# Matmul operands on the left of SBUF, and the norms' two steps a chunk apart, in a two-layer hybrid encoder

## The chip, the cores and the metric

One NeuronCore of a Trainium2 chip runs the whole program. The metric is device time in microseconds (us), from the first to the last instruction of a launch, and the figure for a kernel is the median of its runs.

## What is computed

The reference is an encoder of two layers on 512 tokens of 1024 channels, in float32. Layer 0 mixes the tokens with RWKV-7 and Hyena, layer 1 with neighbourhood attention. Behind each mixer come a gated feed-forward part and a gated per-layer embedding. The parts that the change touches:

```python
def rmsnorm(x, g):
    xf = x.astype(jnp.float32)
    y = xf * lax.rsqrt(jnp.mean(xf * xf, axis=-1, keepdims=True) + EPS)
    return (y * g.astype(jnp.float32)).astype(x.dtype)

def conv_ffn(h, norm_g, w_up, conv_w, conv_b, w_down):
    u = dwconv_centred(rmsnorm(h, norm_g) @ w_up, conv_w, conv_b)
    return (jax.nn.gelu(u[..., :D_FF]) * u[..., D_FF:]) @ w_down

def per_layer_embedding(h, p_i, norm_g, w_gate, w_proj):
    return jax.nn.sigmoid(rmsnorm(h, norm_g) @ w_gate) * (p_i @ w_proj)

# in reference(), for each layer i
    z = rmsnorm(h, na_norm[j]) @ na_w_qkv[j]                      # layer 1's mixer
    h = h + neighbourhood_attention(z, na_q_g[j], na_k_g[j], na_rpb[j]) @ na_w_out[j]
    h = h + conv_ffn(h, ffn_norm[i], ffn_w_up[i], ffn_conv_w[i], ffn_conv_b[i], ffn_w_down[i])
    h = h + per_layer_embedding(h, p[i], ple_norm[i], ple_w_gate[i], ple_w_proj[i])
```

## The kernel before

**Stages.** `run` (L475) does layer 0's mixer (`mixer0`), then the second part of its output projection (`outproj0`, L1551), `ffn(0)`, `ple(0)`, `mixer1`, `ffn(1)` and `ple(1)`. The residual stream stays in SBUF as eight tiles `h` of 128 channels by 512 tokens. The mixer of layer 0 works in 59 slabs `w` of 2,080 bytes per partition and leaves `h_d` in DRAM, from which `outproj0` loads `h` (L1553).

**Every product in float32r.** Each operand is split in two parts, high and low, and a product is three matmuls (`mm3`, L370): high by high, high by low, low by high. `split` (L361) makes the high part on ScalarE and the low part on VectorE. Of the activations the parts are `xh`/`xl` (normed input), `hh`/`hl` (the feed-forward's hidden tiles) and `oh`/`ol` (attention's output); of the weights `whi`/`wlo`.

**Weights in chunks.** `load_split` (L375) brings 512 KB from DRAM into `wraw`, casts `whi` on ScalarE (L364) and subtracts `wlo` on VectorE (L356). Three buffers each. `gemm` (L384) takes four output tiles at a time and, per chunk, two row tiles of weights: 4 x 2 x 3 = 24 matmuls of 512 columns. The weights are stationary and the activations stream. In `gemm_tok` (L1631, attention's queries, keys and values) it is the other way round: `xh`/`xl` are stationary and `whi`/`wlo` stream.

**The norms.** `norm` (L435) splits `gain * h` at once, and 1/rms is applied where a product leaves PSUM (`u<-g,rstd`). The factor is computed while the first product runs, by `then()`, which `gemm` calls after its second chunk (L406): four matmuls add the squares `nacc` over the channels, VectorE scales (`rv`), GpSimd takes the power (`rr`), ScalarE spreads the result along a row (`rex`), TensorE transposes it four times (L431) and ScalarE copies `rstd` (L459). In `mixer1` the sums stand ahead of the first product (L1673 to L1677) and no transposes are needed.

**What sets the order.** Tile's scheduler puts each engine's instructions in one order ahead of time, and each engine runs its own strictly in that order. Loads go through SyncE's queue (SP), in one order too: a load whose place in SBUF is still being read holds up all that stand behind it.

**Where tiles lie.** Pools are stacks that grow from the two ends of SBUF; `side` says from which. Worked out from the sizes and the order in which pools open, in KB per partition from the bottom, with what the change makes of it:

| tiles | before | changed |
|---|---|---|
| `xh`, `xl` | 19.8 to 51.8 | the same |
| `wraw` | 51.8 to 63.8 | 212.0 to 224.0 |
| `whi` | 63.8 to 75.8 | 51.8 to 63.8 |
| `wlo` | 75.8 to 87.8 | 63.8 to 75.8 |
| `oh`/`ol`, eight pairs in turn | 101.7 to 133.7 | 75.8 to 107.8 |
| `hh`, twelve | 160.0 to 184.0 | 75.8 to 99.8 |
| `hl`, twelve | 184.0 to 208.0 | 99.8 to 123.8 |
| `h` | 208.0 to 224.0 | 183.8 to 199.8 |
| norm's tiles (`nsq`, `nacc`, `rstd`, `rex`) | 87.8 to 100.0 | 199.8 to 212.0 |
| slabs `w` of the mixer of layer 0 | 104.1 to 224.0 | the same |

The stages share this space one after the other, and a tile's first writer waits for the last reader of what lay there.

Of the kernel before, what the change touches and what calls it, by code (L numbers as in the profile page):

```python
# [10 lines left out]
F32 = mybir.dt.float32  # L11
# [21 lines left out]
# ---------------------------------------------------------------- layout of the weights  # L33
# [14 lines left out]
# row tiles of layer 0's output projection: those of its early part, and the others  # L48
# [20 lines left out]
def _kc(n):  # L69
    """Row tiles of weights in a chunk of n column tiles."""  # L70
    return (8, 4, 2, 2)[n - 1]
# [13 lines left out]
# columns of the packed per-channel parameters: name -> number of columns  # L85
# [32 lines left out]
# ---------------------------------------------------------------- constants of the shapes  # L118
# [23 lines left out]
def _constants():  # L142
# [18 lines left out]
    # transforms at the frequencies (2f+1)pi/1024, f < 256; even and odd times apart, which gives those of 511 - f  # L161
# [4 lines left out]
    fwd = parts.reshape(4, 4, P, 2, P)  # part, tile of times, time, fc, f  # L166
    c["dft_f"] = np.ascontiguousarray(fwd.transpose(3, 2, 0, 1, 4)).reshape(2, P, 2048)
    inv = parts.transpose(0, 2, 1).reshape(4, 2, P, S)  # part, fc, f, time
    c["dft_i"] = np.ascontiguousarray(inv.transpose(1, 2, 0, 3)).reshape(2, P, 2048)
    # filter features and decay window  # L170
# [10 lines left out]
def _rpb_table(rpb):  # L181
    """Relative position bias as each (16-column query block, head) reads it, both by columns of the grid;
    -1e30 outside the window."""
# [16 lines left out]
    t = np.stack(out, axis=2).reshape(8, 2, P, 3, 256)  # pair, head, q, table, key  # L200
# [3 lines left out]
# ---------------------------------------------------------------- the kernel  # L204
class Pace:
    """Estimates of when what is written so far will have run. The order in which the rest is written follows them;
    nothing that is computed depends on them."""
# [16 lines left out]
    def area(x):  # L224
        """Name, first and last row, first and last column."""
# [16 lines left out]
    def ready(self, tiles):  # L242
        """When all that is written into the tiles so far is there."""
        self.update()
        return max((math.inf if self.pending.get(n) else max(self.done.get(n, {}).values(), default=0.0)
                    for n in map(self.name, tiles)), default=0.0)

    def after(self, marks, area, e, own):
        """The end of the accesses in marks to an area, seen by engine e; those of its own count only if own."""
# [10 lines left out]
    # TensorE runs at half its clock after a stretch of this many us in which it streamed less than so many columns  # L260
# [5 lines left out]
    def density(self, t):  # L266
        """Columns streamed in the last TICK us before t."""
# [48 lines left out]
class Kern:  # L316
# [5 lines left out]
    # -- helpers  # L322
# [38 lines left out]
    def split(self, h, l, src, scale=None):  # L361
        """h + l = src (* scale), each in float32r."""
# [12 lines left out]
    def load_split(self, src, width, dt=F32):  # L375
        """One chunk of weights: from DRAM and into its two parts."""
# [7 lines left out]
    def gemm(self, wname, g, k0, k1, xs, evac, then=None):  # L384
        """then: what goes in between after two chunks of weights."""
# [6 lines left out]
        for kc in range(k0, k1, KC):  # L392
# [13 lines left out]
            if then is not None and kc == k0 + KC:  # L406
                then()

    def rsqrt_rows(self, pool, srcs, col, scale, eps):
        """For each of srcs [128 channels, tokens]: 1 / sqrt(scale * (sums over the channels of col) + eps),  # L410
        back on all of those channels, in PSUM."""
        nc = self.nc
        n = col.shape[1]
        w = 4 * n
        ps = self.pm.tile([P, len(srcs) * w], F32, name="m")
        for i, src in enumerate(srcs):
            for t in range(4):
                o = i * w + t * n
                self.mm(ps[:, o:o + n], src[:, t * P:(t + 1) * P], col)
        v = pool.tile([P, len(srcs) * w], F32, name="rv", bufs=2)  # L420
        r = pool.tile([P, len(srcs) * w], F32, name="rr", bufs=2)
        nc.vector.tensor_scalar(out=v, in0=ps, scalar1=scale, scalar2=eps, op0=ALU.mult, op1=ALU.add)
        self.tt(r, v, self.epsc[:, 4:4 + len(srcs) * w], ALU.pow, nc.gpsimd)
        out = []
        for i in range(len(srcs)):
            ex = pool.tile([P, 4, n, P // n], F32, name="rex")
            rv = r[:, i * w:(i + 1) * w].rearrange("p (t n) -> p t n", n=n).unsqueeze(3)
            nc.scalar.copy(ex, rv.to_broadcast([P, 4, n, P // n]))
            po = self.pm.tile([P, S], F32, name="m")
            for t in range(4):  # L430
                nc.tensor.transpose(po[:, t * P:(t + 1) * P], ex[:, t].rearrange("p n x -> p (n x)"), self.cst("ident"))  # L431
            out.append(po)
        return out

    def norm(self, h, gain):  # L435
        """Splits gain * h into float32r parts; returns them, the tile of 1 / rms per token, on all partitions,
        and what computes that."""
# [17 lines left out]
        rstd = self.pn.tile([P, S], F32, name="rstd", bufs=1)  # L455

        def then():
            ps, = self.rsqrt_rows(self.pn, [acc], self.cst("one"), 1.0 / D, EPS)
            nc.scalar.copy(rstd, ps)  # L459
# [1171 lines left out]
    def gemm_tok(self, wname, g, xs, evac):  # L1631
# [3 lines left out]
        for kc in range(0, KT, 2):  # L1635
            off = (g * KT + kc) * P * S
            hi, lo = self.load_split(self.a[wname][off:off + 2 * P * S].rearrange("(p a) -> p a", p=P), 1024)
            for t in range(4):
# [7 lines left out]
                if kc == KT - 2:  # L1646
                    evac(t, ps[t])
# [199 lines left out]
```

## Time and profile before

| | |
|---|---|
| runs shown | 1638.45, 1636.56 and 1633.0 us, median 1636.56 |
| profiled execution: its own time and its span | 1633.0 us and 1633.0 us |
| TensorE busy | 94% of the span |
| VectorE, ScalarE, GpSimd busy | 64%, 42%, 21% |
| HBM | 121 GB/s over the span |

The profile lists for each engine what it ran and for how long, and what ended the idle time before it. The profiled execution is the fastest of the runs shown, 3.6 us (0.2%) under the median. A matmul's listed duration is from its start to its modelled end, and the next one starts before that end: what a matmul costs is the distance from its start to the start of the next. PE stands for TensorE's matmuls, PEld for its weight loads, DVE for VectorE, ACT for ScalarE, POOL for GpSimd, SP for SyncE.

### The profile page before, as it was taken

The numbers are of one execution on the slowest core, as the hardware profiler recorded it, in microseconds if no ns is written. First come the engines' busy times: TensorE is split into PE (matmuls) and PEld (weight loads), VectorE is DVE, ScalarE is ACT, GpSimd is POOL, SyncE is SP. The second block draws the span as 40 slices with busy tenths as digits, with TensorE's granted clock in tenths as the row PEclk, the third lists the DMA queues.
The fourth block names the chain that finished last, engine by engine and source line by source line (L and its number), as shares of the span: only waits on it lengthen the run. The fifth ranks groups of instructions, "written<-read, shape, count | busy, mean of one in ns | idle before, by whom it ended". The sixth has DMA issues, their size and how long they took to land.

```text
span 1633.0 us, 24094 instructions
## 1 busy us (share of the span) xinstructions
PE 1541.6 (94%) x9296; PEld 1216.2 (74%) x9296; DVE 1047.9 (64%) x1740; ACT 681.0 (42%) x1082; POOL 341.3 (21%) x286
## 2 busy tenths in 40 slices
PE   7998798979898999999999989999999999999997
PEld 4675576766667888888888778777777888888886
DVE  7579868876876677534684664565666665276654
ACT  6464224333514544313443553565554442144432
POOL 3585525533721200000001322011030000000020
PEclk9999899899999999999999999999999999999999
DMA  6455638465764232222322433323112332322341
GB/s 202 136 141 137 188 105 237 136 215 157 232 214 167 100 103 90 96 99 90 103 91 96 137 116 103 106 83 123 66 65 78 103 104 90 98 88 93 110 142 65
DMA packets 116308, 200.13 MB, mean 123 GB/s; under 512 B 27729, under 2 KB 57297, under 8 KB 116194
## 3 DMA queue, kind: packets, MB, share of 16 engines
q1 hardware_dynamic: 116194, 198.59, 37.9%
q8 instruction: 73, 1.20, 0.3%
q14 instruction: 41, 0.34, 0.1%
HBM read 166.04 MB, written 30.93 MB: 121 GB/s over the span
## 4 chain that ended last, share of the span: by engine, by line
PE 76%; DVE 11%; issue 5%; ACT 3%; DMA 2%; POOL 2%; SPq 2%; POOLq 0%; DVEq 0%; ACTq 0%
PE g L350 60%; PE b L350 11%; DVE w L356 4%; DVE w L353 3%; PE m L350 1%; PE s L350 1%; PE m L1792 1%; ACT w L359 1%; POOL w L356 1%; DVE w L1168 1%; POOL rr L356 0%; ACT oh L364 0%; DVE ol L356 0%; DMA ch_d<-w 0%; POOL nacc L356 0%
## 5 line engine op out<-in xcount | busy, mean ns | idle before, releaser
L356 DVE TENSOR_TENSOR wlo<-wraw,whi 128x1024 fp32r<-128x1024 f32 x186 | 235.6, 1268 | 334.7 <-ACT whi L364 334.5
L364 ACT CAST whi<-wraw 128x1024 fp32r<-128x1024 f32 x186 | 194.2, 1044 | 426.8 <-PE g L350 410.2
L350 PE MATMUL g<-xh,whi 128*128 128x512 f32 x872 | 341.5, 392 | 5.4 <-ACT whi L364 5.4
L350 PE MATMUL g<-xl,whi 128*128 128x512 f32 x872 | 340.5, 390 | 0.0
L350 PE MATMUL g<-xh,wlo 128*128 128x512 f32 x872 | 340.3, 390 | 0.0
L356 POOL TENSOR_TENSOR w<-w 128x512 fp32r<-128x512 f32 (+2 forms) x142 | 184.0, 1317 | 166.7 <-ACT w L584 95.8
L350 PEld LDWEIGHTS g<-xh,whi 128*128 128x128 f32 x872 | 164.2, 188 | 41.2 <-ACT whi L364 5.6
L350 PEld LDWEIGHTS g<-xh,wlo 128*128 128x128 f32 x872 | 164.1, 188 | 34.9 <-DVE wlo L356 0.8
L350 PEld LDWEIGHTS g<-xl,whi 128*128 128x128 f32 x872 | 164.3, 188 | 33.7
L350 PE MATMUL b<-xh,w 128*128 128x512 f32 x464 | 172.4, 427 | 7.4 <-ACT xh L359 7.3
L356 POOL TENSOR_TENSOR nacc<-nsq 128x512 f32<-128x512 f32 x5 | 9.3, 1865 | 779.8 <-ACT nsq L359 779.8
L350 PE MATMUL b<-w 64*64 64x64 f32 (+6 forms) x1884 | 131.2, 271 | 17.5 <-DVE w L353 7.5
L350 PE MATMUL g<-hh,wlo 128*128 128x512 f32 x352 | 139.0, 395 | 0.0
L350 PE MATMUL g<-hl,whi 128*128 128x512 f32 x352 | 139.0, 395 | 0.0
L350 PE MATMUL g<-hh,whi 128*128 128x512 f32 x352 | 138.9, 395 | 0.0
L353 DVE SCALAR_TENSOR_TENSOR c<-u,prm,c 128x511 f32<-128x511 f32 x176 | 126.6, 748 | 6.9 <-ACT c L359 6.3
L350 PEld LDWEIGHTS b<-w 64*64 64x64 f32 (+4 forms) x1884 | 94.6, 142 | 44.1 <-POOL w L356 10.4
L350 PEld LDWEIGHTS b<-xh,w 128*128 128x128 f32 x464 | 91.6, 197 | 36.8 <-ACT xh L359 8.0
L359 ACT ACTIVATE c<-u,prm 128x512 f32<-128x512 f32 x88 | 70.0, 817 | 71.4 <-DVE u L356 71.4
L350 PE MATMUL b<-xl,w 128*128 128x512 f32 x232 | 95.7, 413 | 1.6 <-DVE xl L353 1.4
L356 DVE TENSOR_TENSOR w<-w 128x512 f32<-128x512 f32 (+16 forms) x127 | 88.8, 708 | 3.8 <-DMA w<-hw_d 1.0
L356 DVE TENSOR_TENSOR u<-g,rstd 128x512 f32<-128x512 f32 x104 | 71.5, 687 | 14.2 <-PE g L350 13.4
(178 smaller groups left out, 2344.0 us busy)
## 6 DMA issues: line engine op xcount, KB each, us to landing
wraw<-in_up SPq DMA_DIRECT2D x88, 512.0 KB, 3.5
wraw<-in_down SPq DMA_DIRECT2D x44, 512.0 KB, 3.4
w<-in_mix_w_in SPq DMA_DIRECT2D x52, 256.0 KB, 3.8
wraw<-in_na_w_qkv SPq DMA_DIRECT2D x24, 512.0 KB, 3.5
x<-ch_d SPq DMA_DIRECT2D x16, 640.0 KB, 5.9
ch_d<-w SPq DMA_DIRECT2D x64, 128.0 KB, 2.7
wraw<-in_gate SPq DMA_DIRECT2D x16, 512.0 KB, 3.5
tab<-in_rpb SPq DMA_DIRECT2D x8, 768.0 KB, 4.3
```

The costliest lines, as they stand in the source:

```text
L350: return self.nc.tensor.matmul(out, lhsT, rhs, start=start, stop=stop)
L353: return self.nc.vector.scalar_tensor_tensor(out=out, in0=in0, scalar=scalar, in1=in1, op0=op0, op1=op1)
L356: return (eng or self.nc.vector).tensor_tensor(out=out, in0=in0, in1=in1, op=op)
L359: return self.nc.scalar.activation(out=out, in_=in_, func=func, **kw)
L364: self.nc.scalar.copy(h, src)
L1168: nc.vector.tensor_reduce(out=x[:, i, 0:i], in_=tv, axis=AX.X, op=ALU.add)
L1792: nc.tensor.transpose(pst[:, i], sc[:, i // 2, (i % 2) * P:(i % 2 + 1) * P], ident)
```

## The change

Tiles that matmuls read lie on the left: `hh`/`hl` and `oh`/`ol` move into left pools of their own, directly above `whi`/`wlo`. Raw weights and the norm's tiles move to the right end. The norm's work comes in two steps: `sums` (sums, `rv`, `rr`) after the second chunk, `spread` (`rex`, transposes, `rstd`) after the third. In `mixer1` the sums move from ahead of the first product to behind its second chunk. Comments also go; nothing else changes.

```diff
-    def gemm(self, wname, g, k0, k1, xs, evac, then=None):
+    def gemm(self, wname, g, k0, k1, xs, evac, then=()):
+        then = deque(then)
...
-            if then is not None and kc == k0 + KC:
-                then()
+            if then and kc > k0:
+                then.popleft()()
...
     def norm(self, h, gain):
...
-        def then():
-            ps, = self.rsqrt_rows(self.pn, [acc], self.cst("one"), 1.0 / D, EPS)
-            nc.scalar.copy(rstd, ps)
-        return (lambda k: xs[k]), rstd, then
+        def sums():
+            ps = self.pm.tile([P, 4], F32, name="m")
+            for t in range(4):
+                self.mm(ps[:, t:t + 1], acc[:, t * P:(t + 1) * P], self.cst("one"))
+            self.rsqrt(r, ps, 1.0 / D, EPS)
+        def spread():
+            ex = self.pn.tile([P, 4, P], F32, name="rex")
+            nc.scalar.copy(ex, r.unsqueeze(2).to_broadcast([P, 4, P]))
+            po = self.pm.tile([P, S], F32, name="m")
+            for t in range(4):
+                nc.tensor.transpose(po[:, t * P:(t + 1) * P], ex[:, t], self.cst("ident"))
+            nc.scalar.copy(rstd, po)
+        return (lambda k: xs[k]), rstd, (sums, spread)
...
     def gemm_pools(self, st, bufs, side):
-        self.wraw = self.pool(st, "wraw", bufs=bufs, side=side)
+        self.wraw = self.pool(st, "wraw", bufs=bufs, side="right")
...
-                self.pn = self.pool(st, "pn", side="left")
+                self.pn = self.pool(st, "pn", side="right")
...
     def ffn(self, l):
             pf = self.pool(st, f"ff{l}", side="right")
+            px = self.pool(st, f"hid{l}", bufs=12, side="left")
...
-                            hh = pf.tile([P, S], F32R, name="hh", bufs=12)
-                            hl = pf.tile([P, S], F32R, name="hl", bufs=12)
+                            hh = px.tile([P, S], F32R, name="hh")
+                            hl = px.tile([P, S], F32R, name="hl")
...
-    def gemm_tok(self, wname, g, xs, evac):
+    def gemm_tok(self, wname, g, xs, evac, then=None):
...
+            if then is not None and kc == 2:
+                then()
     def mixer1(self):
             pa = self.pool(st, "pa", side="right")
+            po = self.pool(st, "po", side="left")
...
-            ps = self.pm.tile([P, 4], F32, name="m")
-            for t in range(4):
-                self.mm(ps[:, t:t + 1], acc[:, t * P:(t + 1) * P], self.cst("one"))
             rstd = pa.tile([P, 4], F32, name="rstd")
-            self.rsqrt(rstd, ps, 1.0 / D, EPS)
-            oh = [(pa.tile([P, S], F32R, name=f"oh{k}"), pa.tile([P, S], F32R, name=f"ol{k}")) for k in range(KT)]
+            def sums():
+                ps = self.pm.tile([P, 4], F32, name="m")
+                for t in range(4):
+                    self.mm(ps[:, t:t + 1], acc[:, t * P:(t + 1) * P], self.cst("one"))
+                self.rsqrt(rstd, ps, 1.0 / D, EPS)
+            oh = [(po.tile([P, S], F32R, name=f"oh{k}"), po.tile([P, S], F32R, name=f"ol{k}")) for k in range(KT)]
...
-                qk, vv = self.qkv(pa, half, lambda k: xs[k], rstd)
+                qk, vv = self.qkv(pa, half, lambda k: xs[k], rstd, sums if half == 0 else None)
```

The built order moves at three kinds of places. On TensorE, at each of the four norms of `ffn` and `ple` (here `ffn(0)`, third chunk of the first product), before:

```order
L350 MATMUL m<-con,nacc 128x1 x4
L350 MATMUL g<-xh_5938,whi 128x512
L350 MATMUL g<-xl_5939,whi 128x512
L350 MATMUL g<-xh_5938,wlo 128x512
L350 MATMUL g<-xh_5942,whi 128x512
L350 MATMUL g<-xl_5943,whi 128x512
L350 MATMUL g<-xh_5942,wlo 128x512
L350 MATMUL g<-xh_5938,whi 128x512
L431 MATMUL m<-con,rex 128x128 x4
```

and now, from the end of the third chunk on:

```order
L350 MATMUL g<-xh_5945,whi 128x512
L350 MATMUL g<-xl_5946,whi 128x512
L350 MATMUL g<-xh_5945,wlo 128x512
L444 MATMUL m<-con,rex 128x128 x4
L350 MATMUL g<-xh_5949,whi 128x512
```

The sums stay where they were; seven matmuls stood between them and the transposes (the third chunk's first seven), now all 24 of that chunk do. ScalarE copies `rstd` one cast of `whi` later. On TensorE in `mixer1`, in the second chunk of the first product of `qkv`, before:

```order
L350 MATMUL g<-whi,xl_8884 128x512
L350 MATMUL g<-whi,xh_8879 128x512
L350 MATMUL m<-con,nacc 128x1 x4
L350 MATMUL g<-wlo,xh_8879 128x512
L350 MATMUL g<-whi,xl_8880 128x512
```

and now, at that chunk's end:

```order
L350 MATMUL g<-wlo,xh_8890 128x512
L350 MATMUL g<-whi,xl_8891 128x512
L350 MATMUL m<-con,nacc 128x1 x4
L350 MATMUL g<-whi,xh_8894 128x512
L350 MATMUL g<-wlo,xh_8894 128x512
```

The sums have moved behind the chunk's other eleven matmuls. On SP's queue at the end of `mixer0`, before:

```order
L1455 DMA w<-s_d_77 128x512
L378 DMA wraw<-in_mix_w_out_b 128x1024 x2
L1553 DMA h_5731<-h_d_130 128x512
L1553 DMA h_5732<-h_d_131 128x512
```

and now:

```order
L1441 DMA w<-s_d_77 128x512
L1539 DMA h_5731<-h_d_130 128x512
L1539 DMA h_5732<-h_d_131 128x512
L1539 DMA h_5733<-h_d_132 128x512
L1539 DMA h_5734<-h_d_133 128x512
L1539 DMA h_5735<-h_d_134 128x512
L1539 DMA h_5736<-h_d_135 128x512
L1539 DMA h_5737<-h_d_136 128x512
L1539 DMA h_5738<-h_d_137 128x512
L378 DMA wraw<-in_mix_w_out_b 128x1024 x2
```

The eight loads of `h` now go ahead of the first two chunks of weights of `outproj0`. Further on, the eight loads `pj` of each `ple` go out among the last loads of the feed-forward's second product instead of among those of `ple`'s own weights. The orders of VectorE and GpSimd stay as they were.

## Rows read from the trace of the kernel before

**Rows 1.** Page, parts 1 and 4: busy time by engine; the chain that ended last.

```profile
PE 1541.6 (94%) x9296; PEld 1216.2 (74%) x9296; DVE 1047.9 (64%) x1740; ACT 681.0 (42%) x1082; POOL 341.3 (21%) x286
...
PE 76%; DVE 11%; issue 5%; ACT 3%; DMA 2%; POOL 2%; SPq 2%; POOLq 0%; DVEq 0%; ACTq 0%
```

**Rows 2.** Windows by stage: length, busy us of PE, PEld, DVE, ACT, POOL; clock.

```profile
0.00:504.00 504.00, 436.56 (x4161) 323.79 (x4161) 388.23 (x726) 203.55 (x388) 247.13 (x230) 0.94 0.57 173
504.00:946.00 442.00, 439.61 (x1921) 359.41 (x1922) 264.02 (x322) 179.11 (x222) 32.19 (x19) 0.99 0.32 108
946.00:1212.00 266.00, 254.96 (x1416) 197.45 (x1415) 153.76 (x393) 141.92 (x278) 40.09 (x25) 0.99 0.28 92
1212.00:1633.00 421.00, 410.52 (x1803) 335.58 (x1801) 241.91 (x303) 156.41 (x196) 21.86 (x13) 0.99 0.29 97
```

**Rows 3.** Timeline at `ffn(0)`'s norm: start, duration, instruction, [idle before, releaser].

```profile
544.58 0.95 PE L350 MATMUL m<-con,nacc 128*128 128x1 f32 x8
545.81 1.94 POOL L356 TENSOR_TENSOR rr<-rv,epsc 128x4 f32<-128x4 f32 x1 [2.48 <-DVE rv L422]
547.78 0.62 ACT L428 COPY rex<-rr 128x512 f32<-128x512 f32 x1 [2.18 <-POOL rr L356]
548.45 0.66 PE L431 MATMUL m<-con,rex 128*128 128x128 f32 x4 [1.18 <-ACT rex L428]
```

**Rows 4.** The tile `rex`, whole run: who waited for it (us, times).

```profile
  PE m L431: 4.7, 4
```

**Rows 5.** Timeline around the sums of `mixer1`.

```profile
954.11 0.39 PE L350 MATMUL g<-whi,xh 128*128 128x512 f32 x1
957.82 1.94 POOL L356 TENSOR_TENSOR nacc<-nacc,nsq 128x512 f32<-128x512 f32 x1 [1.22 <-ACT nsq L359]
959.81 1.86 PE L350 MATMUL m<-con,nacc 128*128 128x1 f32 x8 [5.31 <-POOL nacc L356]
961.54 0.77 PE L350 MATMUL g<-wlo,xh 128*128 128x512 f32 x1
```

**Rows 6.** Windows there, and around a 3.04 us wait in `mixer0`.

```profile
959.20:966.00 6.80, 6.19 (x19) 5.22 (x20) 1.80 (x2) 0.00 (x0) 1.58 (x2) 0.50 0.69 258
446.70:450.60 3.90, 0.90 (x14) 0.70 (x16) 3.77 (x5) 0.00 (x0) 3.90 (x4) 1.00 1.04 352
450.60:454.00 3.40, 3.39 (x35) 2.34 (x31) 3.23 (x7) 0.27 (x1) 2.18 (x3) 0.50 1.03 369
```

**Rows 7.** Windows in an up product (`xh`, `xl` stream) and a down product (`hh`, `hl`).

```profile
560.00:660.00 100.00, 100.00 (x442) 82.36 (x441) 67.22 (x88) 44.46 (x57) 0.00 (x0) 1.00 0.29 95
667.40:734.60 67.20, 67.20 (x289) 54.09 (x288) 28.94 (x35) 16.23 (x19) 0.00 (x0) 1.00 0.29 95
```

**Rows 8.** Matmuls into `g`: count, duration ns min/median/max, first and last start.

```profile
L350 PE MATMUL g<-xh,whi x872: 387/389/796, 504.0 to 1624.0; 128*128 128x512 f32 x175
L350 PE MATMUL g<-hh,whi x352: 392/394/398, 667.4 to 1577.7; 128*128 128x512 f32 x176
L350 PE MATMUL g<-whi,xh x192: 387/389/628, 946.0 to 1126.9; 128*128 128x512 f32 x192
```

**Rows 9.** Timeline: 48 `oh`/`ol` matmuls, the first, and what follows the last.

```profile
1201.29 0.40 PE L350 MATMUL g<-oh,whi 128*128 128x512 f32 x1
...
1212.44 0.40 PE L350 MATMUL g<-xh,whi 128*128 128x512 f32 x1
```

**Rows 10.** Timeline at the end of `mixer0` and the start of `outproj0`.

```profile
501.65 0.69 DVE L356 TENSOR_TENSOR w<-w 128x512 f32<-128x512 f32 x1
503.99 0.80 PE L350 MATMUL g<-xh,whi 128*128 128x512 f32 x1 [5.38 <-ACT whi L364]
505.05 1.04 ACT L364 CAST whi<-wraw 128x1024 fp32r<-128x1024 f32 x1 [1.11 <-DMA wraw<-in_mix_w_out_b]
```

**Rows 11.** Window from there on.

```profile
504.00:508.60 4.60, 4.56 (x10) 3.16 (x11) 2.42 (x2) 1.04 (x1) 0.00 (x0) 0.50 0.96 340
```

**Rows 12.** Page, part 6: a load of weights, KB each, us to landing.

```profile
wraw<-in_up SPq DMA_DIRECT2D x88, 512.0 KB, 3.5
```

More of the change, by code (lines that the diff above doesn't have):

```diff
@@ L405, in gemm @@
                     evac(j, ps[j])
-            if then is not None and kc == k0 + KC:
-                then()
[L409 to L416, printed above, removed]
-            for t in range(4):
[L418 to L433, printed above, removed]
+            if then and kc > k0:
+                then.popleft()()
     def norm(self, h, gain):
@@ L455, in norm @@
         rstd = self.pn.tile([P, S], F32, name="rstd", bufs=1)
-        def then():
-            ps, = self.rsqrt_rows(self.pn, [acc], self.cst("one"), 1.0 / D, EPS)
-            nc.scalar.copy(rstd, ps)
-        return (lambda k: xs[k]), rstd, then
+        r = self.pn.tile([P, 4], F32, name="rr", bufs=2)
+        def sums():
[11 more added lines that the diff above has]
+        return (lambda k: xs[k]), rstd, (sums, spread)
     def conv3(self, out, u, w, b):
@@ L1594, in ffn @@
                         self.gemm(f"up{l}", i * 2 + half, 0, KT, xs, lambda j, ps, h=half, e=evac: e(j, ps, h),
-                                  then if i == half == 0 else None)
+                                  then if i == half == 0 else ())
                 k0 = i0 * 4
@@ L1625, in evac @@
                         nc.sync.dma_start(out=self.out[i], in_=self.h[i])
-                self.gemm(f"gate{l}", g, 0, KT, xs, evac, then if g == 0 else None)
+                self.gemm(f"gate{l}", g, 0, KT, xs, evac, then if g == 0 else ())
             for k in range(KT):
                 self.dump(f"p{l}_{k}", self.h[k])
-    def gemm_tok(self, wname, g, xs, evac):
+    def gemm_tok(self, wname, g, xs, evac, then=None):
         K, groups = WEIGHTS[wname]
@@ L1672, in mixer1 @@
                     acc = new
-            ps = self.pm.tile([P, 4], F32, name="m")
-            for t in range(4):
-                self.mm(ps[:, t:t + 1], acc[:, t * P:(t + 1) * P], self.cst("one"))
             rstd = pa.tile([P, 4], F32, name="rstd")
-            self.rsqrt(rstd, ps, 1.0 / D, EPS)
-            oh = [(pa.tile([P, S], F32R, name=f"oh{k}"), pa.tile([P, S], F32R, name=f"ol{k}")) for k in range(KT)]
+            def sums():
[4 more added lines that the diff above has]
+            oh = [(po.tile([P, S], F32R, name=f"oh{k}"), po.tile([P, S], F32R, name=f"ol{k}")) for k in range(KT)]
             for half in range(2):
-                qk, vv = self.qkv(pa, half, lambda k: xs[k], rstd)
+                qk, vv = self.qkv(pa, half, lambda k: xs[k], rstd, sums if half == 0 else None)
                 for m in range(half * 4, half * 4 + 4):
@@ L1697, in rsqrt, with qkv @@
         self.tt(out, v[:, :n], self.epsc[:, 4:4 + n], ALU.pow, self.nc.gpsimd)
-    def qkv(self, pa, half, xs, rstd):
+    def qkv(self, pa, half, xs, rstd, then):
         nc = self.nc
@@ L1723, in qkv @@
         for x in range(3):
-            self.gemm_tok("na_w_qkv", half * 3 + x, xs, lambda t, ps, x=x: evac(t, ps, x))
+            self.gemm_tok("na_w_qkv", half * 3 + x, xs, lambda t, ps, x=x: evac(t, ps, x), then if x == 0 else None)
         for t in range(3):
```

## The prediction
> **What bounds the kernel now.** I read the page first. TensorE is busy for 94% of the span, and the chain of work that ended last lies on it for 76%, on VectorE for 11% [rows 1]. The windows by stage then show where TensorE has room [rows 2]: it is busy for 437 of 504 us in layer 0's mixer, 440 of 442 in the first feed-forward and embedding, 255 of 266 in attention, 411 of 421 behind it. The change alters nothing inside layer 0's mixer, so the rest is at stake, and there TensorE sets the end: only a wait in its own order, or a matmul that takes less time, moves it. So I looked in the timeline for its waits at the places where the change moves something, and for matmuls of one shape that cost unequal time. There are three finds: a wait ahead of the transposes of four norms [rows 3, 4], one ahead of attention's sums [rows 5, 6], and a slower beat where the streaming tile lies on the right [rows 7 to 9]. At a fourth place, the first weights behind the mixer, the change may lose [rows 10 to 12].
>
> **Transposes behind a full chunk.** The sums start at 544.58, the transposes that need their result at 548.45 [rows 3]. Between them lie GpSimd's power (1.94 us) and ScalarE's spreading (0.62), and on TensorE seven matmuls. It runs out of those and waits; over the run it does so at four norms, 4.7 us in all counted from modelled ends [rows 4]. Counted by starts, the sums (0.95 us) and seven matmuls of 0.227 us (441 starts in 100 us, the one already running left out [rows 7]) fill 2.54 of the 3.87 us, which leaves 1.33 a norm. In the new order 24 matmuls stand between, 5.4 us; with the sums 6.4 us against a chain of 3.9. The wait goes with 2.5 us to spare: 4 x 1.33 = **5.3 us saved**. ScalarE's copy of `rstd` now stands behind a cast of `whi` (1.04 us [rows 10]) that starts as the third chunk ends. With a spreading copy's 0.62 us for its own length it is done some 1.7 us later, while the fourth chunk's first output leaves after the transposes (0.66) and six matmuls (1.36), 2.0 us later. I cost this at nothing; without that cover VectorE would start on the outputs later, not TensorE.
>
> **Attention's sums behind the second chunk.** TensorE stops at 954.34 (954.11 and one beat) and takes the sums at 959.81, when GpSimd has added the last squares (957.82 and 1.94) [rows 5]. It comes out of the wait at half clock, 1.2 GHz, until 966.0 [rows 6]; the 19 instructions there are the eight passes of the sums and the chunk's other eleven matmuls, which so end their beat at about 966.2. In the new order these eleven come first, 11 x 0.227 = 2.5 us, until 956.84. GpSimd's chain is no earlier, so TensorE still waits until 959.8, now 3.0 us: that chain is what is late next, not weights. At full clock the sums take 0.95 us and the next chunk starts at 960.7, 5.5 us sooner than 966.2; if the clock falls for as long as before, only the 2.5 us of moved work remain. The nearest row is a wait of 3.04 us in layer 0's mixer (0.90 us busy of 3.90), behind which came 3.4 us at half clock [rows 6]. That costs half of itself, 1.7: 5.5 - 1.7 = **3.8 us saved**, with 2.5 and 5.5 as ends.
>
> **The hidden tiles on the left.** In an up product 441 matmuls start in 100 us, 226.8 ns each; in a down product 288 start in 67.20 us, 233.3 ns each: the same shape, both at the full 2.4 GHz, no idle time [rows 7]. Their durations differ likewise, 389 against 394 ns, and hold for all 352 of a kind [rows 8]. What differs is where the streaming tile lies: `xh` below 52 KB, `hh` and `hl` above 160. `whi` and `wlo`, up to 87.8 KB, stream at 389 ns too [rows 8]; `oh` and `ol`, from 101.7 KB up, take (1212.44 - 1201.29)/48 = 232.3 ns [rows 9]. So the beat changes somewhere between 88 and 102 KB. The new `hh` lies at 76 to 100 KB, the new `hl` at 100 to 124, where `oh` was slow. I take `hh` as fast and `hl` as slow: of 1,056 matmuls 704 stream `hh`, and 704 x 6.5 ns = **4.6 us saved**. The ends are nothing (it is not the place) and 1,056 x 6.5 = 6.9 us (all of the left is fast). Of 192 matmuls on `oh`/`ol` three quarters lie below 100 KB, at 5.5 ns 0.8 us, but most fill gaps of attention: **0.5 us saved**, ends 0 and 1.1.
>
> **The first weights behind the mixer.** `wraw` now lies at 212 to 224 KB, on slabs of the mixer. In the built program its first load waits for VectorE's product `w<-w` of 501.65, done at 502.34 [rows 10], and stands in SP's queue behind eight loads of `h`, whose slabs are free by then. Before, its place was free long ahead, and ScalarE's own order held the cast. A load of 512 KB lands 3.5 us after issue [rows 12], at 505.8, and with the cast of 1.04 the first matmul starts at 506.9 instead of 503.99: **3.0 us lost**. The ends: 1.9 (a landing in 2.4 us), and 4.7, if the half clock that follows here [rows 11] lasts 3.4 us longer and takes half of that besides.
>
> **What else moves.** Loads of `pj` go out some chunks sooner, between loads of weights for which three buffers stand: nothing, and if one held the queue, a chunk (5.4 us) covers it. VectorE and ScalarE read `wraw` from the far end: if they took longer, their idle 33 and 56 us of 100 in an up product would cover it [rows 7]: nothing.
>
> **Sum.** -5.3 - 3.8 - 4.6 - 0.5 + 3.0 = -11.2 us. The profiled execution took 1633.0 us, span and own time alike, so 1621.8; it lies 3.56 under the median of 1636.56, and against that I forecast **1625.4 us** (-0.7%).
>
> **Rivals.** *The place does not matter* (0.15). For it: `hh` and `xh` stream in different products, which differ by more than the place. Against it: two products with other partners, attention's output and the down product, are both slow, and both kinds of low tile are fast. Without 4.6 and 0.5 it gives 1630.5 us. In a sentence apart: the Trainium skill ("TensorE: Matmul & The Clock Gate", Back-to-back issue gap) prices a matmul by columns and clock alone, about 216 ns for 512, wherever its operands lie, and by "SBUF — State Buffer" (Who interferes with whom) TensorE waits for no other engine's accesses; by these the move saves nothing, and this trace, with two beats of 227 and 233 ns, does not agree with the first.
>
> *All of the left is fast* (0.15): the slow `oh` owed its beat to something in its stage. Then 2.3 us more for `hl` and 0.3 for `ol`: 1622.8.
>
> *It ends slower: the left end is crowded* (0.05). Hidden tiles, `whi` and `wlo` are then written where TensorE reads, and the up products could fall to the beat of 233 as well. 3 x 872 matmuls use `xh`/`xl` [rows 8]; at 6.5 ns that is 17 us, with 4.6 and 0.5 not gained: 1625.4 + 5.1 + 17 = 1647.5. It decides from 6.1/0.0065 = 940 slowed matmuls on. Against it: `whi` and `wlo` are written on the left all the time already, at a beat of 227.
>
> *It does not do what it says* (0.08): the four waits come back as a later one, `rstd` late behind its cast and TensorE without a free bank of PSUM. Then the 5.3 us are not gained: 1630.7. The 2.5 us to spare speak against it.
>
> **Chances.** The forecast's own case has 0.57. The favourable ends give -5.3 - 5.5 - 6.9 - 1.1 + 1.9 = -16.9, 1619.7, the bad ones -5.3 - 2.5 + 4.7 = -3.1, 1633.5; with some 1 us for the scatter of a median the range is 1618 to 1634, and leaves out the slower case and the worst of the others. A measurement of this kernel tells 0.3% (4.9 us) from no change: faster means under 1631.7, which takes in the forecast's case, the fast left and more than half of the two rivals near 1630.6 (0.82); the same has 0.12, slower 0.06.
>
> **What would show it.** Afterwards TensorE's wait for `rex` (4.7 us) should be gone; the sums of `mixer1` should wait about 3 us for GpSimd, with a shorter half clock behind; in down products `hh` should show 389 ns and `hl` 394, and 288 matmuls take 66.0 us; the first matmul behind the mixer should start near 506.9. I am wrong if the down products still take 67.2 us, if the up products leave 226.8 ns a matmul, or if the first weights come over 5 us later.

## The result, and the profile after

| | before | changed |
|---|---|---|
| median of the runs, us | 1635.64 (1633.0 to 1638.45) | 1627.4 (1623.7 to 1629.27) |
| ratio of the two, 95% interval | | 0.9941, 0.992 to 0.9961 |
| profiled execution: span, us | 1633.0 | 1627.5 |

The change gains 8.2 us, 0.6%; by the interval between 6.4 and 13.1. (In every run here with both figures a run's own time is 1.7 to 2.2 us above its span, the changed kernel's 1629.27 to 1627.5. The span of 1633.0 us before therefore belongs, as it seems, to a run of about 1635 us and not to the fastest one. The forecast goes from the median and is not touched by this.)

To see where they come from I cut both traces, and those of the experiments, at the same matmuls and measured from start to start. A norm's piece runs from its sums to the next product that a trace marks clearly (the down product, attention's projections, the end).

| piece, us | before | changed | norms_only | right_offset | left_offset | wraw_left | both_moved | sums_third |
|---|---|---|---|---|---|---|---|---|
| `mixer0`, to its last matmul | 498.3 | 503.8 | 499.6 | 499.2 | 496.1 | 500.0 | 495.8 | 497.7 |
| from there to the first matmul of `outproj0` | 5.7 | 11.4 | 5.7 | 5.7 | 11.1 | 5.7 | 5.7 | 5.7 |
| the four pieces behind a norm's sums | 324.8 | 319.3 | 319.4 | 325.1 | 319.3 | 319.4 | 321.3 | 319.3 |
| attention's first projection to its first scores | 76.8 | 73.1 | 74.5 | 76.9 | 73.1 | 73.1 | 73.0 | 69.3 |
| the down products of both layers | 246.4 | 239.6 | 246.4 | 239.7 | 246.4 | 239.7 | 239.6 | 239.7 |
| all else | 481.0 | 480.3 | 482.0 | 480.8 | 479.9 | 480.5 | 485.1 | 481.2 |
| span | 1633.0 | 1627.5 | 1627.5 | 1627.2 | 1625.8 | 1618.3 | 1620.5 | 1612.8 |

The first line is no effect of any edit in the table. These eight kernels have layer 0's mixer instruction for instruction and slab for slab alike, and it ends between 495.8 and 503.8 us. So one profile per kernel cannot show a few microseconds in the span. The norms and the down products can: where nothing in them was changed they repeat to 0.3 us. ("All else" holds `outproj0`, 40.0 to 41.9 us by the clock that it meets.) Without the mixer's 5.5 us the changed kernel's profile gains 11.0 us.

**Busy time, chain and stages**, from the page of the changed kernel (answering to [rows 1]) and from its windows (length; busy us of PE, PEld, DVE, ACT, POOL; clock; DMA; to be held against [rows 2]):

```profile
PE 1535.4 (94%) x9296; PEld 1217.3 (75%) x9296; DVE 1048.9 (64%) x1740; ACT 679.9 (42%) x1082; POOL 340.6 (21%) x286
...
PE 66%; ACT 1%; DVE 1%; DMA 0%; POOL 0%; issue 0%; SPq 0%; DVEq 0%; POOLq 0%; ACTq 0%
```

```profile
503.80:515.20 11.40, 0.29 (x3) 0.08 (x2) 5.26 (x10) 3.61 (x6) 0.00 (x0) 0.74 0.80 279
515.20:950.80 435.60, 435.56 (x1921) 359.49 (x1922) 263.81 (x321) 178.70 (x222) 32.05 (x19) 1.00 0.31 104
950.80:1213.20 262.40, 253.90 (x1418) 196.55 (x1417) 153.91 (x393) 141.92 (x279) 41.31 (x25) 0.99 0.29 94
1213.20:1627.50 414.30, 406.18 (x1801) 335.40 (x1799) 241.66 (x303) 155.94 (x196) 21.52 (x13) 0.99 0.29 98
```

The chain's shares add up to 68% only, because it is followed back no further than the load of `wraw` at 507.86; they can't be held against those of before. From 515.2 on TensorE has no gap left in the first feed-forward part. In front of it stands a hole of 11.4 us. TensorE's whole busy time fell by 6.2 us at the same number of instructions: part of the gain is no wait that went, but matmuls that take less.

**Norms.** The timeline at `ffn(0)`, the same place as [rows 3]:

```profile
555.61 0.95 PE L350 MATMUL m<-con,nacc 128*128 128x1 f32 x8
556.84 1.94 POOL L356 TENSOR_TENSOR rr<-rv,epsc 128x4 f32<-128x4 f32 x1 [2.55 <-DVE rv L1689]
558.81 0.62 ACT L441 COPY rex<-rr 128x512 f32<-128x512 f32 x1 [2.18 <-POOL rr L356]
562.01 0.60 PE L444 MATMUL m<-con,rex 128*128 128x128 f32 x4
```

The spreading copy is done at 559.43, the transposes come at 562.01 without a wait ahead of them. The four pieces fell by 1.43, 1.36, 1.39 and 1.37 us: 5.5.

**Attention's sums**, as in [rows 5, 6], the timeline and then three windows:

```profile
962.70 1.94 POOL L356 TENSOR_TENSOR nacc<-nacc,nsq 128x512 f32<-128x512 f32 x1 [1.26 <-ACT nsq L359]
964.69 1.05 PE L350 MATMUL m<-con,nacc 128*128 128x1 f32 x8 [2.90 <-POOL nacc L356]
965.60 0.48 PE L350 MATMUL g<-whi,xh 128*128 128x512 f32 x1
```

```profile
964.70:966.60 1.90, 1.90 (x12) 1.74 (x13) 1.76 (x3) 0.00 (x0) 0.51 (x1) 1.00 0.34 140
966.60:970.00 3.40, 3.40 (x9) 2.61 (x8) 0.58 (x1) 0.00 (x0) 1.46 (x1) 0.50 0.93 340
970.00:975.00 5.00, 5.00 (x23) 4.15 (x22) 0.95 (x1) 1.66 (x2) 0.00 (x0) 1.00 0.37 139
```

A wait of 2.9 us is left, and 3.4 us at half clock behind it. The piece gained 3.7 us.

**Hidden tiles.** The matmuls into `g` (count, ns min/median/max) and a down product's window, as in [rows 7, 8]:

```profile
L350 PE MATMUL g<-hh,whi x352: 389/389/501, 677.0 to 1573.6; 128*128 128x512 f32 x176
L350 PE MATMUL g<-hl,whi x352: 389/389/395, 677.2 to 1573.8; 128*128 128x512 f32 x176
```

```profile
677.00:742.40 65.40, 65.40 (x289) 53.98 (x288) 28.91 (x35) 16.19 (x18) 0.00 (x0) 1.00 0.30 97
```

`hl` is at 389 ns as well as `hh`: 288 matmuls in 65.4 us, 227 ns each. The four products gained 6.8 us.

**The first weights.** The timeline of SP, ScalarE and TensorE behind the mixer, and the load of `wraw`, as in [rows 10]:

```profile
501.87 5.89 SPq L1539 DMA_DIRECT2D h<-h_d  x8
507.86 1.34 SPq L378 DMA_DIRECT2D wraw<-in_mix_w_out_b  x3
514.10 1.04 ACT L364 CAST whi<-wraw 128x1024 fp32r<-128x1024 f32 x1 [5.63 <-DMA wraw<-in_mix_w_out_b]
515.20 0.80 PE L350 MATMUL g<-xh,whi 128*128 128x512 f32 x1 [11.11 <-ACT whi L364]
```

The load goes out when the mixer's last product is done (507.12 and 0.69), as forecast; the eighth load of `h` went out just ahead of it, at 507.38. But it is there 6.2 us later, not 3.5.

### The profile page after: what moved, and what is told of

Same layout as the page of the kernel before. It is cut to its first block, busy times and chain, and to the rows that moved or that the text cites. A ratio compares the mean times of both kernels' runs of the same rounds, so it can differ in the third digit from the quotient of the medians.

```text
span 1627.5 us, 24082 instructions
## 1 busy us (share of the span) xinstructions
PE 1535.4 (94%) x9296; PEld 1217.3 (75%) x9296; DVE 1048.9 (64%) x1740; ACT 679.9 (42%) x1082; POOL 340.6 (21%) x286
## 4 chain that ended last, share of the span: by engine, by line
PE 66%; ACT 1%; DVE 1%; DMA 0%; POOL 0%; issue 0%; SPq 0%; DVEq 0%; POOLq 0%; ACTq 0%
PE g L350 62%; PE s L350 1%; PE m L350 1%; PE m L1785 1%; ACT oh L364 0%; DVE ol L356 0%; DMA wraw<-in_mix_w_out_b 0%; PE m L1736 0%; POOL nacc L356 0%; DVE u L356 0%; ACT xh L359 0%; ACT nsq L359 0%; DVE w L353 0%; DVE h L356 0%; SPq L1539 0%
## 5 line engine op out<-in xcount | busy, mean ns | idle before, releaser
L350 PE MATMUL g<-xh,whi 128*128 128x512 f32 x872 | 341.7, 392 | 11.1 <-ACT whi L364 11.1
L350 PE MATMUL b<-xh,w 128*128 128x512 f32 x464 | 176.6, 437 | 8.9 <-ACT xh L359 8.9
```

Of the source, the lines that this page charges most:

```text
L350: return self.nc.tensor.matmul(out, lhsT, rhs, start=start, stop=stop)
```

## The experiments

**Side or offset?** Two rivals were left open by the result: `hl` at 99.8 to 123.8 KB is quick where `oh` at 101.7 to 133.7 was slow [rows 9], so no border in height can divide them. What else the move changed is where the tiles start within a few hundred bytes, worked out from the sizes and the order of the pools. `xh`, `whi` and `wlo` start 288 bytes past a multiple of 512. `hh` and `hl` started 480 past one, `oh` and `ol` 160; in the changed kernel all start at 288. Two kernels part the side from the offset.

`left_offset`, the changed kernel with the old offset on the left:

```diff
+            sp = self.pool(st, f"sp{l}", side="left").tile([P, 48], F32, name="sp")
+            nc.gpsimd.memset(sp, 0.0)
             px = self.pool(st, f"hid{l}", bufs=12, side="left")
```

> The changed kernel with 192 bytes put under the hidden tiles, which stay left: hh and hl move from byte 77600 and 102176 to 77792 and 102368, and so from 288 to 480 bytes past a multiple of 512, where they lay on the right before the change. By 'the side decides' nothing changes: 288 matmuls of a down product take 65.4 us and a matmul on hh or hl 389 ns, as in the changed kernel. By 'the offset decides' the old beat is back: 67.2 us, 394 ns, and 2 x (1.8 + 1.6) = 6.8 us more in all.

`right_offset`, the kernel before with the new offset on the right:

```diff
+            sp = self.pool(st, f"sp{l}", side="right").tile([P, 48], F32, name="sp")
+            nc.gpsimd.memset(sp, 0.0)
             pf = self.pool(st, f"ff{l}", side="right")
```

> The kernel before with 192 bytes put beside its feed-forward pool on the right: hh and hl stay on the right (160 to 208 KB), but lie 288 bytes past a multiple of 512, as xh, whi and wlo do, and no longer 480. By 'the side decides' the down products stay at 67.2 us and 394 ns, and the time at 1635.6. By 'the offset decides' they fall to 65.4 us and 389 ns, and the time by 6.8 us to 1628.8.

The matmuls into `g` and the first down product's window in `left_offset`:

```profile
L350 PE MATMUL g<-hh,whi x352: 392/394/398, 668.6 to 1571.9; 128*128 128x512 f32 x176
```

```profile
668.60:735.80 67.20, 67.20 (x290) 54.10 (x289) 28.90 (x35) 16.20 (x19) 0.00 (x0) 1.00 0.29 95
```

and in `right_offset`:

```profile
L350 PE MATMUL g<-hh,whi x352: 389/389/500, 668.4 to 1571.7; 128*128 128x512 f32 x176
```

```profile
668.40:733.80 65.40, 65.40 (x289) 53.96 (x288) 28.89 (x35) 16.24 (x19) 0.00 (x0) 1.00 0.29 97
```

On the left at the old offset the tiles are slow, on the right at the new one quick. The side does nothing; the offset does it all. `right_offset` took 1628.97 us, ratio 0.9952 (0.9934 to 0.997): 192 bytes that nothing reads are worth 7 us. `left_offset` took 1627.62 in its one run, not 6.8 us more than the changed kernel, because its mixer ended at 496.1 and not 503.8; its down products show the 6.8.

**Which offset, and within how many bytes?** Either 288 is quick by itself, or the streaming tile and the weights must agree. `both_moved` moves weights and hidden tiles together and leaves `xh` behind. It and the next two start from `wraw_left` (below).

```diff
         self.wraw = self.pool(st, "wraw", bufs=bufs, side=side)
+        sp = self.pool(st, "spw", side="left").tile([P, 48], F32, name="spw")
+        self.nc.gpsimd.memset(sp, 0.0)
         self.whi = self.pool(st, "whi", bufs=bufs, side=side)
```

> The kernel of the run wraw_left (1619.3 us) with 192 bytes put under the split weights: whi, wlo, hh, hl, oh and ol all move from 288 to 480 bytes past a multiple of 512, xh and xl stay at 288. By 'streaming tile and weights must lie at one offset' the down products stay at 389 ns and 226.8 ns a matmul, since both sides moved together, and the up and gate products, whose sides now differ, fall to 394 ns and 233.3: 3 x 872 x 6.5 ns = 17 us more, and up to 3.5 us more in attention's projections, 1636 to 1640 us. By 'the offset 288 itself is the quick one for the streaming tile' the up products stay at 226.8 ns and the down products go to 233.3: 6.8 us more, 1626 us.

`steps_a` and `steps_b` put a tile of another size under the hidden tiles of each layer:

```diff
+            n = (64, 128)[l]
+            sp = self.pool(st, f"sp{l}", side="left").tile([P, n], F32, name="sp")
```

> The kernel of wraw_left with 256 bytes put under the hidden tiles of the first layer and 512 under those of the second. What counts may be the offset within 64, 128, 256, 512 or 2048 bytes. 128 is out already: oh and ol lay 128 bytes off before the change and were slow. By 256 both layers keep 389 ns; by 512 the first layer is slow (394 ns, 67.2 us a product of 288) and the second is not; by 2048 both are slow.

> The kernel of wraw_left with 1024 bytes put under the hidden tiles of the first layer and 32 under those of the second. By 'the offset within 256 or 512 bytes' the first layer keeps 389 ns and 65.4 us a product of 288 matmuls; by 2048 it goes to 394 ns and 67.2 us. The second layer shows whether a shift of 32 bytes is enough: 394 ns if it must be equal, 389 if only a coarser difference counts.

In `both_moved`, windows of an up and of a down product:

```profile
560.00:660.00 100.00, 100.00 (x438) 81.87 (x437) 64.51 (x85) 41.75 (x52) 0.00 (x0) 1.00 0.31 100
665.60:730.90 65.30, 65.30 (x289) 53.97 (x288) 28.84 (x35) 16.08 (x18) 0.00 (x0) 1.00 0.29 97
```

In `steps_b`, the first down product of layer 0 (1024 bytes) and of layer 1 (32 bytes):

```profile
667.70:733.10 65.40, 65.40 (x289) 53.98 (x288) 28.90 (x35) 16.23 (x18) 0.00 (x0) 1.00 0.29 97
1336.10:1403.30 67.20, 67.20 (x289) 53.95 (x288) 28.95 (x35) 16.27 (x19) 0.00 (x0) 1.00 0.28 94
```

In `steps_a`, the same two (256 and 512 bytes):

```profile
669.30:734.80 65.50, 65.50 (x290) 54.04 (x289) 28.95 (x35) 16.35 (x19) 0.00 (x0) 1.00 0.30 97
1339.00:1404.40 65.40, 65.40 (x289) 53.98 (x288) 28.94 (x35) 16.26 (x18) 0.00 (x0) 1.00 0.29 97
```

It is agreement: in `both_moved` the down products stay quick at 480 bytes, and the up products, left at 288 with weights at 480, slow down, to 100/437 = 228.8 ns. Tiles 256, 512 and 1024 bytes apart agree, tiles 32 apart do not. So what counts is the difference within 256 bytes: at 0 a matmul takes 226.8 ns, at 32 and 192 (`hh` before) 233.3, at 128 (`oh` before) 232.3, and at 64, the up products of `both_moved`, 228.8.

How much slower, the difference alone does not say. The first product behind the mixer in `both_moved` (`outproj0`) has `xh` and `whi` 64 bytes apart too, and there a matmul takes (540.54 - 507.64)/141 = 233.3 ns. In attention's projections of that kernel the two change roles, `whi` streams and `xh` stands, and it takes (1010.08 - 959.68)/216 = 233.3:

```profile
507.64 0.40 PE L350 MATMUL g<-xh,whi 128*128 128x512 f32 x1
540.54 0.40 PE L350 MATMUL g<-xh,whi 128*128 128x512 f32 x1
959.68 0.39 PE L350 MATMUL g<-whi,xh 128*128 128x512 f32 x1
1010.08 0.39 PE L350 MATMUL g<-whi,xh 128*128 128x512 f32 x1
```

In `norms_only`, where `oh` lies as before, 128 bytes off, the same 48 matmuls take (1209.70 - 1198.50)/48 = 233.3 ns instead of 232.3. Why one difference gives two beats is open.

I had priced the up products of `both_moved` at 6.5 ns instead of 2; the pieces behind its mixer grew by 6.4 us in all, not 17 to 20. Attention's first piece did not grow, though its matmuls took 6.5 ns more: the wait for GpSimd was 2.55 us there, and TensorE came out of it at full clock, where `wraw_left` has a wait of 2.9 us and some 3.4 us at half clock. The sums, and a window from there on:

```profile
954.48 1.05 PE L350 MATMUL m<-con,nacc 128*128 128x1 f32 x8 [2.55 <-POOL nacc L356]
```

```profile
954.50:958.00 3.50, 3.50 (x19) 3.04 (x20) 2.35 (x3) 0.00 (x0) 1.97 (x1) 1.00 0.55 181
```

The runs of `both_moved` gave 1628.66 us, ratio 0.9957 (0.9944 to 0.9971).

**Was it the place of `wraw` that delayed the first weights?**

```diff
-        self.wraw = self.pool(st, "wraw", bufs=bufs, side="right")
+        self.wraw = self.pool(st, "wraw", bufs=bufs, side=side)
```

> The changed kernel with the raw weights (wraw) left again, everything else as changed. My account of the lost 6.0 us is that the first load of wraw waits for the last product of the mixer and then lands 6.2 us late behind eight loads of h. Then from the mixer's last matmul to the first of the output projection pass 5.4 us and not 11.4, the cast of whi waits for no load there, and the time is 1627.4 - 6.0 = 1621.4. Rival: the loads of h ahead in SP's queue are what holds the weights, wherever they lie; then the gap stays above 10 us and the time at 1627. hh and hl move up by 12 KB, to 88 to 136 KB, at the same offset of 288 bytes: by 'the offset decides' and by 'the side decides' they stay at 389 ns; by a border in height above 124 KB, hl rises to 394 ns and the down products by a third of 6.8 us.

The timeline of ScalarE and TensorE there:

```profile
504.53 1.04 ACT L364 CAST whi<-wraw 128x1024 fp32r<-128x1024 f32 x1
505.62 0.80 PE L350 MATMUL g<-xh,whi 128*128 128x512 f32 x1 [5.38 <-ACT whi L364]
```

The cast waits for no load, the idle time is 5.38 us as before [rows 10], and the hole between the two stages is 5.7 us again. It is the place, but not the place alone: with `wraw` on the left its first two loads also stand ahead of the eight of `h` in SP's queue again (488.72 and 503.27, the first `h` at 503.66). No run has the old place with the new order, so the rival is not ruled out: whether the slab or the eight loads ahead held the load back is not told apart. The kernel takes 1619.28 us, ratio 0.9896 (0.9876 to 0.9915), 8 us less than the changed one (medians of two sets of runs), of which this piece holds 5.7. `hl`, now up to 136 KB, stays at 389 ns.

**Are the two-step norms alone worth 9.2 us?** `norms_only` is the kernel before with the new `norm`, `gemm` and the new place of attention's sums, and every tile where it was.

> The kernel before with the norms in two steps alone, every tile where it lay before the change. Expected from the comparison of the two traces: 5.5 us gone at the four norms and 3.7 in attention's projections, down products unchanged at 67.2 us, the gap behind the mixer 5.4 us: 1635.6 - 9.2 = 1626.4. Rival: part of the gain at the norms came from their tiles, which lie on the right in the changed kernel (the adds of the squares or the power would be quicker there); then a wait for rex of up to 1.3 us a norm is left and the time is 1627 to 1632.

It takes 1627.38 us, ratio 0.9942 (0.9923 to 0.9962). The four norms gain 5.4 us, all of what the change gains there, so the tiles' places have no part in it. Attention's piece gains 2.3 and not 3.7. Its windows show the difference:

```profile
959.30:961.10 1.80, 1.77 (x9) 1.77 (x9) 1.06 (x1) 0.00 (x0) 0.00 (x0) 0.50 0.37 150
961.10:965.00 3.90, 3.90 (x10) 3.08 (x11) 1.33 (x2) 0.00 (x0) 1.96 (x1) 0.50 0.87 326
```

After the same wait the clock had already fallen when the sums came and stayed down for longer; in the changed kernel the sums still ran at full clock. In `steps_a`, with the same order here, the piece takes 74.3 us, in `steps_b` 73.1. So the gain of this part is 2.3 to 3.7 us, by when the clock falls; what decides that is not shown.

**Is what is left of that wait to be had?** `sums_third` is `wraw_left` with the sums a chunk later.

```diff
-            if then is not None and kc == 2:
+            if then is not None and kc == 4:
```

> The kernel of wraw_left with attention's sums behind the third chunk of weights and not the second. My account says that in the changed kernel TensorE waits 3.0 us there for GpSimd's last add (done 9 us after the first matmul of the projection, the second chunk 11 us after it with its sums) and runs 3.4 us at half clock behind: 3.0 + 1.7 = 4.7 us to be had, 1619.3 - 4.7 = 1614.6, no wait at the sums and no half clock behind them. Rival: rstd is then late for the fourth chunk's outputs and TensorE waits for banks of PSUM instead; then at most 1 to 2 us are gained.

The timeline of TensorE and a window from there on:

```profile
956.96 0.39 PE L350 MATMUL g<-whi,xl 128*128 128x512 f32 x1
957.19 0.95 PE L350 MATMUL m<-con,nacc 128*128 128x1 f32 x8
957.99 0.49 PE L350 MATMUL g<-whi,xh 128*128 128x512 f32 x1
```

```profile
958.00:975.00 17.00, 17.00 (x77) 14.06 (x77) 7.76 (x14) 7.60 (x12) 7.96 (x5) 1.00 0.34 117
```

No wait, and full clock behind it; the piece is 3.8 us shorter than in `wraw_left`, of the 4.7 expected. At 1614.86 us, ratio 0.9873 (0.9856 to 0.989), this is the fastest kernel of the study, 20 us below the kernel before (1634.75 in the same set) and 12.5 below the changed one's 1627.4.

**Can the mixer have quick matmuls too?** Its slabs are 2,080 bytes long and start at every multiple of 32, while `xh` and `xl` stay at 288. Slabs of 2,304 bytes keep one offset, but then only 53 fit. `slabs_53` is the control with 53 of the old length:

```diff
-    SLABS = 59
+    SLABS = 53
-        return self.sl.tile([P, 520], dt, name="w")[:, 0:n]
+        return self.sl.tile([P, 576], dt, name="w")[:, 0:n]
```

(the second pair in `slabs_even` only; a tile of 192 bytes ahead of the pool, left out here, is in both, so that the two differ in the length of the slabs alone)

> A control for the next run: the kernel of sums_third (1614.9 us) with 53 slabs in layer 0's mixer and not 59, each 2080 bytes long as before, so that they lie at all multiples of 32 bytes. It shows what six slabs fewer cost by themselves; the runs so far bear on it with nothing. Expected: 1615 to 1620 us, and matmuls of the mixer with 512 columns 232 ns apart, as before.

> The kernel of slabs_53 with slabs 2304 bytes long and their pool 192 bytes lower, instruction for instruction in the same order: every slab now lies 32 bytes past a multiple of 256, as xh and xl do (288 = 256 + 32). By 'streaming tile and weights must agree within 256 bytes' the mixer's 696 matmuls of 512 columns on xh and xl go from 232.0 to 226.8 ns, and most of the 240 on slabs alone, at most 936 x 5.2 ns = 4.9 us; some of them fill waits, so 2 to 5 us less than slabs_53. Rival: in the mixer the beat has another cause (the stores and loads beside it, GpSimd's traffic), since in the trace of before no pair of offsets there was clearly quick; then it stays at 232 ns and the time at that of slabs_53.

One unbroken stretch of 29 such matmuls, its first, its tenth and its last one, in `slabs_53`:

```profile
89.21 0.40 PE L350 MATMUL b<-xl,w 128*128 128x512 f32 x1
91.29 0.39 PE L350 MATMUL b<-xl,w 128*128 128x512 f32 x1
95.71 0.40 PE L350 MATMUL b<-xh,w 128*128 128x512 f32 x1
```

and in `slabs_even`:

```profile
92.38 0.39 PE L350 MATMUL b<-xl,w 128*128 128x512 f32 x1
94.46 0.39 PE L350 MATMUL b<-xl,w 128*128 128x512 f32 x1
98.77 0.39 PE L350 MATMUL b<-xh,w 128*128 128x512 f32 x1
```

Six slabs fewer cost 9.8 us (1624.66; 0.992 to 0.9958 of before), where up to 5 were expected. The even offsets give 4.2 of them back (1620.46; 0.9898 to 0.9931), but from start to start, of matmuls whose next one follows within 260 ns, the beat goes from 232.2 to 229.7 ns, half of the way to 226.8. The intervals overlap a little, so the gain in time is likely, not certain. The stretch shows why the beat stops half-way: its first nine matmuls take 231.1 ns each in both kernels, and only from the tenth on do the two part, (95.71 - 91.29)/19 = 232.6 ns against (98.77 - 94.46)/19 = 226.8. In all but one of the stretches of `slabs_even` with 13 or more such matmuls the quick beat sets in after two to nine; but a stretch of the mixer has only about seven on average.

The last two kernels keep 59 slabs by making only a few of them longer than 2,048 bytes.

The pool `sb` and a tile that sets the offset of the short slabs are left out here:

```diff
+    SLABS, WIDE = 52, 7
+        if n > 512:
+            return self.sb.tile([P, 520], dt, name="w")[:, 0:n]
+        return self.sl.tile([P, 512], dt, name="w")[:, 0:n]
```

> The kernel of sums_third (1614.9 us), in the same order, with the mixer's 59 slabs in two kinds: 52 of 2048 bytes, all 32 bytes past a multiple of 256 as xh and xl are, and 7 of 2080 for the tiles that need more than 512 columns. The run slabs_even gained 4.2 us by offsets, slabs_53 lost 9.8 by six slabs fewer. If only the number of slabs made that loss, 1614.9 - 4.2 = 1610.7 us; if tiles of over 512 columns or the others now wait for a slab of their own kind, part of the loss is back, 1611 to 1620.

> The same with 50 slabs of 2048 bytes and 9 of 2080. It tells which kind runs short: if the short ones, this is slower than slabs_two7; if the wide ones, quicker; 1610.7 us if neither does.

They take 1620.8 us (0.9905 to 0.9935) and 1622.81 (0.991 to 0.9945): 6 and 8 us slower than `sums_third`. Two kinds of slab with the same total cost more than the even offsets give. The runs of the two overlap (1617.17 to 1622.43 and 1617.15 to 1625.61), so which kind runs short is not told.

## Why the prediction was right, and where it was not

The forecast of 1625.4 us lies 2.0 below the median of 1627.4, and it named faster by over 0.3%. It started from a median of 1636.56, the result from 1635.64 with one run more; of the change itself 8.2 of 11.2 us came. Of its five terms three hold, and two are off by 2 to 3 us in opposite directions.

- *Transposes behind a full chunk*, 5.3 us: 5.5. The wait for `rex` is gone at all four norms, and `norms_only` shows that the order alone does it. That `rstd` behind its cast costs TensorE nothing held too: `mixer0` and the wait behind it apart, no piece grew.
- *Attention's sums*, 3.8 us: 3.7, with the wait (2.9 for 3.0) and the shorter half clock as forecast. `norms_only` puts it at 2.3, just below the lower end of 2.5, which stood for a clock that stays down as long as before.
- *The hidden tiles*, 4.6 us: 6.8. **The step that failed is "the beat changes somewhere between 88 and 102 KB".** The two beats were read rightly, and that they belong to where the tile lies. But I ordered the tiles by one coordinate only, the height, and drew a border between the two beats. The tiles' offset within 256 bytes divides them just as well, and was to be worked out from the same addresses; `left_offset` and `right_offset` settle it. So "all of the left is fast" gave the right size for `hl`, and by its number the rival was right, but not by its reason, since a tile on the left can be slow. "The place does not matter" was right of the side and wrong of the price.
- In sentences apart: the Trainium skill ("TensorE: Matmul & The Clock Gate", Back-to-back issue gap) has about 216 ns for a single matmul of 512 columns at full clock; in long stretches here one takes 226.8 to 233.3, so the measurement decides against one price for all. By "SBUF — State Buffer" (Operand start alignment) an operand may start at any multiple of its element size, and the page says that its runs timed nothing; every kernel here starts its tiles at a multiple of 32, and the time is not the same for all.
- *`oh` and `ol`*, 0.5 us: from the first scores to the next up product 189.68 went to 189.33, 0.35. Most of them do fill gaps.
- *The first weights behind the mixer*, 3.0 us lost: 5.7 lost. **The step that failed is "a load of 512 KB lands 3.5 us after issue".** The issue came when forecast. The landing took 6.2 us, since the load is the first of several behind eight loads of `h`; the window from the issue to the cast shows the DMA engines 97 to 99% busy:

```profile
507.80:511.00 3.20, 0.00 (x0) 0.00 (x0) 1.31 (x3) 0.62 (x1) 0.00 (x0) 0.72 0.99 319
511.00:514.10 3.10, 0.00 (x0) 0.00 (x0) 0.00 (x0) 0.00 (x0) 0.00 (x0) 0.50 0.97 380
```

I had taken the 3.5 us from loads of `in_up` in the middle of a product [rows 12]. The right row stood in the trace of before, in its DMA issues from 498 to 516 us:

```profile
h<-h_d SPq DMA_DIRECT2D x8, 256.0 KB, 5.5
wraw<-in_mix_w_out_b SPq DMA_DIRECT2D x3, 512.0 KB, 6.2
```

With it the term would have been 3.0 + 2.7 = 5.7, outside the end of 4.7 that I gave. My own mark for being wrong, first weights over 5 us later, was passed; the time came out right by luck, because the hidden tiles gave 2.2 us more. The favourable end, a landing in 2.4 us, had no row either: the quickest of the loads of `wraw` before took 3.3.

The sum of the five pieces as measured is -5.5 - 3.7 - 6.8 - 0.35 + 5.7 = -10.7 us against -11.2 forecast; the medians differ by 8.2, inside the interval of 6.4 to 13.1. What lies between is of the size of the mixer's scatter, and I have no run that puts it down to anything else.

Of the rivals, the crowded left end did not come: an up product of the changed kernel takes as long as before (108.9 and 109.0 us between two down products). The four waits did not come back in another place. *The place does not matter* and *all of the left is fast* are answered above.

## What to carry to other kernels

When matmuls of one shape show two beats, list the start address of every operand, and look at its remainder as well as its height, before naming a place; then pad one tile by the smallest step and look at one product with long unbroken stretches of matmuls. Price a moved load by the landings at the place where it will go out, not by those of a quiet stretch. And cut the two traces at the same instructions: a piece of the program that nobody touched can differ by more than the change is worth.

## What the runs showed of the hardware that I had not expected

- In an unbroken stretch a matmul of 512 float32r columns on 128 rows takes 226.8 ns when the streaming tile and the stationary one start at the same byte within 256, and 228.8 to 233.3 when they start 32, 64, 128 or 192 bytes apart. One difference can give two beats: at 64 bytes 228.8 in the up products of `both_moved` and 233.3 in its `outproj0`. Only these differences, and only starts at multiples of 32, were tried; what in the chip causes it is not shown.
- It needs no more than a spare tile: 192 bytes brought the kernel before from 1636.23 to 1628.97 us.
- One unchanged stage, layer 0's mixer, ended anywhere from 495.8 to 503.8 us over eight profiles.
- The quick beat does not come at once: in the mixer of `slabs_even` it sets in after two to nine matmuls of a stretch, so short stretches gain little.
- After the same wait of 2.9 us the clock had already fallen when the sums came in `norms_only` and `steps_a`, and fell 1.9 us after they began in the changed kernel; after a wait of 2.55 us, in `both_moved`, it did not fall.
